# Computing the gate and up products of 15 feed-forward column blocks with the weights stationary and the tokens moving

## The chip, the cores and the metric

The kernel runs on one core of a Trainium2 chip. The metric is the device time of one execution in microseconds, the median over several runs. The trace is that of one profiled execution of the same program.

## The reference

One decoder layer on 256 tokens of width 2048, in float32: a SwiGLU feed-forward (FFN1), a token-mixing sub-layer, a second SwiGLU feed-forward (FFN2) and a last RMS norm. What the change touches is the first half of both feed-forwards, whose hidden width is 5632:

```python
def swiglu(h, w_gu, w_down):                       # h: 256 x 2048
    gate, up = jnp.split(h @ w_gu, 2, axis=-1)     # w_gu: 2048 x 11264
    return (jax.nn.silu(gate) * up) @ w_down       # w_down: 5632 x 2048
```

`x = x + 0.5 * mod * swiglu(h, ...)` is done twice, with h = modulate(rms_norm(x)). The scales and shifts of the modulation are products of one vector with a matrix of 2048 x 18432 (the conditioning), whose rows the kernel streams in beside the other work.

## The kernel before

**A product.** Every float32 operand of a large product is split in two fp32r parts, hi and lo, and a product is the sum of three: hi·hi, lo·hi, hi·lo. The activations h lie transposed in SBUF, contraction on the partitions, as `held.hi` and `held.lo` (two tiles, class `Held`, line 341), each 16 contraction steps k of 128 rows by 256 tokens. The weights come in column blocks of 512 (`CH`): `load` (line 309) brings four contraction steps, 1 MB, by one DMA on SP's queue into one of four `raw` buffers; `split` (line 330) makes of half of that (two k, 128 x 1024) `wh` by a cast on ScalarE (line 334) and `wl` by a subtraction on VectorE (line 335), into three rotating buffers each. `products` (line 319) then issues for each k and each half t of the tokens three matmuls:

```python
nc.tensor.matmul(ps, ah[:, j, ts], wh[:, j, :], start=first, stop=False)   # line 326
nc.tensor.matmul(ps, al[:, j, ts], wh[:, j, :], start=False, stop=False)   # line 327
nc.tensor.matmul(ps, ah[:, j, ts], wl[:, j, :], start=False, stop=last)    # line 328
```

The first operand, 128 x 128 of the activations, is stationary; the second, 512 columns of weights, moves. `gemm` (line 383) does so for one column block: 16 k x 2 token halves x 3 = 96 matmuls of 512 columns, into two PSUM banks (`acc_bank`, four of them), tokens on the partitions.

**The feed-forward's first half.** `ffn_up` (line 545) runs over the 11 blocks `ci` of 512 hidden columns. For each it computes the gate product, then the up product, then calls `swiglu_up` (line 525), which for each token half applies Silu to the gate's bank (ScalarE, line 537), multiplies with the up bank (VectorE, line 538) and calls `transpose_to` (line 412): four TensorE transposes of 128 x 128 (line 416) into a bank of another pool (`bank`, two of them) and a copy (line 417) into the tile that the down product reads, where the hidden columns lie on the partitions. So a block has 192 matmuls of 512 columns and eight transposes.

In FFN1 the blocks 0 to 5 go another way (`visit`, line 772: all column blocks grow together while the conditioning arrives), and `ffn_up` does the blocks 6 to 10. In FFN2 the gate product of block 0 (`head`) has been computed within the sub-layer before, and `ffn_up` does the rest of block 0 and the blocks 1 to 10.

**What sets the order.** SP's DMA queue follows the program's order. The order on TensorE, VectorE and ScalarE in these stretches is made by the framework's scheduler, which lets ready work overtake within the dependencies. Every half of a weight block calls `tick`, which now and then issues conditioning passes (line 203, VectorE) and loads of conditioning rows on SP's queue; at the end of an output of the conditioning, `gate_out` (line 266) takes a `bank`, a transpose and a ScalarE multiply. Of the remaining PSUM, two banks (`side_bank`) are used by the token mixing and the square sums, and by nothing in these blocks.

Of the kernel before, what the change touches and what calls it, by code (L numbers as in the profile page):

```python
# [9 lines left out]
F32 = mybir.dt.float32  # L10
F32R = mybir.dt.float32r
AF = mybir.ActivationFunctionType
# [4 lines left out]
P = 128  # L17
S = 256
D = 2048
DFF = 5632  # L20
NT = S // P
KD = D // P
KF = DFF // P
CH = 512
KB = 4
# [51 lines left out]
def layer_kernel(  # L77
# [22 lines left out]
    nc = tc.nc  # L100
    ctx.enter_context(tc.manual_schedule(engines={mybir.EngineType.SP}))
    b_ada = b_ada[0]
    one = ctx.enter_context(tc.tile_pool(name="one", bufs=1))
    raws = ctx.enter_context(tc.tile_pool(name="raws", bufs=RAWS))
    wsp = ctx.enter_context(tc.tile_pool(name="wsp", bufs=3))
# [10 lines left out]
    def nm(s):  # L116
        uid[0] += 1
        return f"{s}_{uid[0]}"

    def acc_bank():  # L120
        return psa.tile([P, CH], F32, tag="acc", name=nm("pa"))

    def bank():
        return psm.tile([P, CH], F32, tag="ps", name=nm("ps"))

    def side_bank():
        return psd.tile([P, CH], F32, tag="pd", name=nm("pd"))

    def t512():
        return tmp.tile([P, CH], F32, tag="t512", name=nm("t"))  # L130
# [4 lines left out]
    def slot():  # L135
        return slots.tile([P, KD * S], F32, tag="slot", name=nm("slot"))
# [154 lines left out]
    def tick():  # L291
        pace["due"] += pace["rate"]
        while pace["due"] >= 1.0:
            pace["due"] -= 1.0
            next(pace["steps"], None)
# [3 lines left out]
    def step():  # L299

        while side:
            try:
                next(side[0])
                break
            except StopIteration:
                side.pop(0)


    def load(w, kb, c0):
        raw = raws.tile([P, KB, CH], F32, tag="raw", name=nm("raw"))  # L310
        nc.sync.dma_start(
            raw,
            w[kb * KB * P : (kb + 1) * KB * P, c0 : c0 + CH].rearrange(
                "(k p) n -> p k n", p=P
            ),
        )
        return raw
# [12 lines left out]
    def split(pool, tag, src, n, hi_engine="act"):  # L330
        k = src.shape[1]
        hi = pool.tile([P, 2, n], F32R, tag=tag + "h", name=nm(tag + "h"))[:, :k, :]
        lo = pool.tile([P, 2, n], F32R, tag=tag + "l", name=nm(tag + "l"))[:, :k, :]
        nc.scalar.copy(hi, src)  # L334
        nc.vector.tensor_sub(lo, src, hi.bitcast(F32))  # L335
        return hi, lo
# [4 lines left out]
    class Held:  # L341


        def __init__(self):
            self.hi = one.tile([P, KD, S], F32R, tag="hh", name=nm("hh"))
            self.lo = one.tile([P, KD, S], F32R, tag="hl", name=nm("hl"))

        def pair(self, k2):
            return self.hi[:, 2 * k2 : 2 * k2 + 2, :], self.lo[:, 2 * k2 : 2 * k2 + 2, :]
# [20 lines left out]
    def gemm_part(act, w, col0s, banks, kb, KT):  # L370

        pairs = [act.pair(kb * 2 + h) for h in range(2)]
        for i, c0 in enumerate(col0s):
            raw = load(w, kb, c0)
            for h in range(2):
                wh, wl = split(wsp, "w", raw[:, 2 * h : 2 * h + 2, :], CH)
                ah, al = pairs[h]
                products(
                    banks[i], ah, al, wh, wl, kb + h == 0, kb * KB + 2 * h + 2 == KT
                )  # L380
                tick()

    def gemm(act, w, col0s, KT=KD):
        banks = [[acc_bank() for _ in range(NT)] for _ in col0s]
        for kb in range(KT // KB):
            gemm_part(act, w, col0s, banks, kb, KT)
            step()
        return banks
# [23 lines left out]
    def transpose_to(dest, src_of, n, ps=None):  # L412

        ps = ps or bank()
        for j in range(n):
            nc.tensor.transpose(ps[:, j * P : (j + 1) * P], src_of(j), ident)  # L416
        nc.any.tensor_copy(dest, ps[:, : n * P])  # L417
# [107 lines left out]
    def swiglu_up(banks_g, banks_u, tiles, ci, parts=None):  # L525

        k0 = ci * KB
        dest = tiles[k0 // KD].rearrange("p (k s) -> p k s", s=S)
        kk = k0 % KD
        for t in range(NT):  # L530
            s = t512()
            g, u = banks_g[t], banks_u[t]
            if parts is not None:
                nc.vector.tensor_add(s, g, parts[0][t])
                nc.vector.tensor_add(parts[1][t], u, parts[1][t])
                g, u = s, parts[1][t]
            nc.scalar.activation(s, g, AF.Silu)
            nc.vector.tensor_mul(s, s, u)
            transpose_to(
                dest[:, kk : kk + KB, t * P : (t + 1) * P],  # L540
                lambda j: s[:, j * P : (j + 1) * P],
                KB,
            )

    def ffn_up(held, w, tiles, first, bg=None):
        for ci in range(first, DFF // CH):
            bg = bg or gemm(held, w, [ci * CH])[0]
            bu = gemm(held, w, [DFF + ci * CH])[0]
            swiglu_up(bg, bu, tiles, ci)
            bg = None  # L550

    ORDERED = {mybir.EngineType.PE, mybir.EngineType.DVE, mybir.EngineType.Activation}

# [141 lines left out]
    held = Held()  # L695
    part = [slot() for _ in range(3)]
    tiles = [slot(), part[0]]
# [62 lines left out]
    banks, moved = {}, set()  # L760
# [60 lines left out]
    place = two_rows()  # L821
    set_pace([(2, None, 0.5), (4, 1, None), (3, None, None)], 154, place, AQ)
    ffn_up(held, gu, tiles, EARLY)
    gate_load(gate, 2)
    wi = w_in[0]
# [144 lines left out]
    for ci in range(4):  # L970
        b = in_chunk(O_SQ + ci * CH)
        for t in range(NT):
            u = t512()
# [10 lines left out]
    for a, off in ((0, O_RQ), (1, O_RK)):  # L984
        for ci in range(2):
            b = in_chunk(off + ci * CH)
            for t in range(NT):
                u = t512()
# [91 lines left out]
    for ci in range(4):  # L1080
        b = in_chunk(O_RG + ci * CH)
        for t in range(NT):
            u = t512()
# [12 lines left out]
    for p in range(2):  # L1096
        sg = first if p == 0 else gates(p)
        c0s = [(2 * p + i) * CH for i in range(2)]
        for g, a, w in ((1, a_swa, w_swa_branch), (0, a_ret, w_ret_branch)):
            banks = gemm(a, w[0], c0s)  # L1100
# [3 lines left out]
        for i in range(2):  # L1104
            for t in range(NT):
                m = sg[:, 0, i, t, :]
                nc.vector.tensor_add(m, m, sg[:, 1, i, t, :])
                k0 = (2 * p + i) * KB
# [12 lines left out]
    tiles = [slot() for _ in range(3)]  # L1121
    set_pace([(8, None, 0.5)], 160, raw_row, 2)
    ffn_up(held, w_ffn2_gu[0], tiles, 0, head)
    gf = one.tile([P, KD * S], F32, tag="hh", name="gf")[:, :D]
    nc.gpsimd.dma_start(gf, norm_final[None, :].broadcast_to([P, D]))
    gate_load(gate, 8)

# [80 lines left out]
```

## Time and profile before

| | us |
|---|---|
| three runs | 2444.01 to 2446.54, median 2445.94 |
| the profiled execution's own time | 2445.11 |
| its span, first to last instruction | 2443.3 |
| TensorE busy | 2398.8 (98%) |
| weight loads busy | 1957.2 (80%) |
| VectorE busy | 1699.8 (70%) |
| ScalarE busy | 1189.8 (49%) |

Times in the profile are microseconds from the first instruction of the span, durations in ns where marked. PE is TensorE's matmuls, PEld its loads of the stationary operand, DVE VectorE, ACT ScalarE, POOL GpSimd. "L335" is line 335 of the kernel. A matmul's recorded duration contains the way through the array, so consecutive ones overlap: the rate is read from the distance of their starts. PEclk is the granted share of TensorE's full clock of 2.4 GHz.

### The profile page before, as it was taken

What the parts mean: (1) busy time and instruction counts of PE and PEld (TensorE: products, weight loads), DVE (VectorE), ACT (ScalarE), POOL (GpSimd) and SP (SyncE); (2) the same over time, 40 slices, a digit from 0 to 9 for tenths busy, and PEclk for the clock granted to TensorE, in tenths of its full rate; (3) what the DMA queues carried; (4) which work ended last, traced back from release to release, by engine and by line L of the source; (5) the groups of instructions that cost most, each with busy time, mean ns of one, the idle gap of its engine ahead of it and who ended that gap; (6) DMA issues with size and microseconds to landing.
All of it is one profiled execution on the core that took longest, in us unless ns stands there. A gap on an engine that the chain in (4) does not pass through costs nothing. (4 is left out here: it accounts for less than half of the span.)

```text
span 2443.3 us, 29136 instructions
## 1 busy us (share of the span) xinstructions
PE 2398.8 (98%) x10910; PEld 1957.2 (80%) x10910; DVE 1699.8 (70%) x2733; ACT 1189.8 (49%) x1614; POOL 5.7 (0%) x14
## 2 busy tenths in 40 slices
PE   7999999999999999999999999999999999999998
PEld 4778888888787777788888888887888888888886
DVE  6898877778877677886666776767655555545656
ACT  6544544444445455554544444456544444444544
POOL 0000000000000000000000000000000000000000
PEclk9999999999999999999999999999999999999999
DMA  9987688888875766666677777755666676665563
GB/s 354 338 333 273 227 310 299 333 304 299 308 264 186 243 210 219 207 217 214 239 262 252 253 254 266 266 189 172 229 227 222 224 244 220 226 225 192 186 200 121
DMA packets 244080, 599.08 MB, mean 245 GB/s; under 512 B 9633, under 2 KB 10017, under 8 KB 225121
## 3 DMA queue, kind: packets, MB, share of 16 engines
q1 hardware_dynamic: 242434, 590.56, 69.0%
q0 software_dynamic: 928, 5.61, 0.6%
q8 instruction: 85, 1.39, 0.2%
q10 hardware_dynamic: 576, 1.05, 0.1%
q14 instruction: 57, 0.47, 0.1%
HBM read 595.06 MB, written 2.12 MB: 244 GB/s over the span
## 5 line engine op out<-in xcount | busy, mean ns | idle before, releaser
L335 DVE TENSOR_TENSOR wl<-raw,wh 128x1024 fp32r<-128x1024 f32 (+1 forms) x828 | 995.7, 1207 | 592.5 <-ACT wh L334 589.5
L334 ACT CAST wh<-raw 128x1024 fp32r<-128x1024 f32 (+1 forms) x828 | 861.2, 1041 | 1031.1 <-PE pa L327 1012.1
L326 PE MATMUL pa<-wh,hh 128*128 128x512 f32 x2224 | 870.0, 392 | 3.4 <-ACT wh L334 2.9
L327 PE MATMUL pa<-wh,hl 128*128 128x512 f32 x2224 | 869.9, 391 | 2.2 <-DVE hl L476 1.8
L328 PE MATMUL pa<-wl,hh 128*128 128x512 f32 x2224 | 803.2, 393 | 4.1 <-DVE wl L335 3.9
L326 PEld LDWEIGHTS pa<-wh,hh 128*128 128x128 f32 x2224 | 417.7, 188 | 93.3 <-ACT wh L334 4.2
L328 PEld LDWEIGHTS pa<-wl,hh 128*128 128x128 f32 x2224 | 415.3, 188 | 95.5 <-DVE wl L335 10.2
L327 PEld LDWEIGHTS pa<-wh,hl 128*128 128x128 f32 x2224 | 418.0, 188 | 89.7 <-DVE hl L476 2.4
L327 PE MATMUL pa<-wh,a 128*128 128x512 f32 x992 | 383.8, 389 | 0.0
L328 PE MATMUL pa<-wl,a 128*128 128x512 f32 x992 | 367.6, 390 | 1.2 <-DVE wl L335 1.1
L326 PE MATMUL pa<-wh,a 128*128 128x512 f32 x992 | 367.2, 390 | 0.4 <-DVE t L519 0.4
L328 PEld LDWEIGHTS pa<-wl,a 128*128 128x128 f32 x992 | 185.7, 188 | 42.3 <-DVE wl L335 4.5
L326 PEld LDWEIGHTS pa<-wh,a 128*128 128x128 f32 x992 | 186.0, 188 | 40.6 <-DVE t L519 1.1
L327 PEld LDWEIGHTS pa<-wh,a 128*128 128x128 f32 x992 | 186.3, 188 | 38.5
L203 DVE CUSTOM_DVE_ANT_0 slot<-slot,cact 128x512 f32<-128x512 f32 (+1 forms) x252 | 192.8, 814 | 31.6 <-DMA slot<-in_w_ada_dram 31.3
L203 DVE CUSTOM_DVE_ANT_0 raw<-raw,cact 128x512 f32<-128x512 f32 (+1 forms) x260 | 167.0, 696 | 38.4 <-DMA raw<-in_w_ada_dram 27.8
L367 DVE TENSOR_TENSOR a<-slot,a 128x512 fp32r<-128x512 f32 x124 | 84.8, 685 | 12.9 <-ACT a L366 12.9
L366 ACT CAST a<-slot 128x512 fp32r<-128x512 f32 x124 | 76.4, 618 | 14.8 <-PE pa L328 14.7
L417 ACT COPY slot<-ps 128x512 f32<-128x512 f32 x80 | 44.7, 586 | 38.5 <-PE ps L416 38.1
L203 DVE DVE_READ_ACCUMULATOR2_ANT sums<- 128x1 f32 x512 | 42.2, 82 | 0.0
L416 PEld LDWEIGHTS ps<-small_c,t 128*128 128x128 f32 x288 | 34.4, 140 | 7.4 <-ACT slot L955 0.7
L416 PE MATMUL ps<-small_c,t 128*128 128x128 f32 x288 | 40.1, 273 | 0.0
(161 smaller groups left out, 965.7 us busy)
## 6 DMA issues: line engine op xcount, KB each, us to landing
raw<-in_w_ffn_gu_dram SPq DMA_DIRECT2D x152, 1024.0 KB, 5.2
raw<-in_w_in_dram SPq DMA_DIRECT2D x104, 1024.0 KB, 5.2
raw<-in_w_ffn_down_dram SPq DMA_DIRECT2D x88, 1024.0 KB, 5.2
slot<-in_w_ada_dram SPq DMA_DIRECT2D x76, 1024.0 KB, 7.6
raw<-in_w_ada_dram SPq DMA_DIRECT2D x64, 1024.0 KB, 4.9
raw<-in_w_ffn_gu_dram SPq DMA_DIRECT2D x24, 768.0 KB, 6.8
raw<-in_w_swa_branch_dram SPq DMA_DIRECT2D x16, 1024.0 KB, 5.3
raw<-in_w_ret_branch_dram SPq DMA_DIRECT2D x16, 1024.0 KB, 5.3
```

Of the source, the lines that this page charges most:

```text
L203: nc.vector.tensor_tensor_reduce(out=w[:, at], in0=w[:, at], in1=cact[:, at], scale=1.0, scalar=0.0, op0=ALU.mult, op1=ALU.add, accum_out= ...
L326: nc.tensor.matmul(ps, ah[:, j, ts], wh[:, j, :], start=first, stop=False)
L327: nc.tensor.matmul(ps, al[:, j, ts], wh[:, j, :], start=False, stop=False)
L328: nc.tensor.matmul(ps, ah[:, j, ts], wl[:, j, :], start=False, stop=last)
L334: nc.scalar.copy(hi, src)
L335: nc.vector.tensor_sub(lo, src, hi.bitcast(F32))
L366: nc.scalar.copy(hi, v)
L367: nc.vector.tensor_sub(lo, v, hi.bitcast(F32))
L416: nc.tensor.transpose(ps[:, j * P : (j + 1) * P], src_of(j), ident)
L417: nc.any.tensor_copy(dest, ps[:, : n * P])
```

## The change

`Held` becomes one tile, `both`, with hi and lo side by side, so that for a given k the 256 tokens of hi and the 256 of lo can move as one operand of 512 columns. A new function `gemm_turned` computes a column block transposed: for each k and each of the four groups `o` of 128 weight columns, the group of `wh` is stationary and hi and lo move together (512 columns, one bank); then the same group of `wl` is stationary and hi moves (256 columns, added to the bank's first half). Loads, splits and ticks keep their places. Hidden columns then lie on the partitions, as the down product wants them, and the transposes fall away. The two halves of each bank are added on the way out: a ScalarE copy of the second half, a VectorE addition of the first, and then Silu (gate) or the product with the gate (up), each on 128 x 256. The gate uses the four `acc` banks, the up product two `bank`s and two `side_bank`s. The 15 blocks are 6 to 10 of FFN1 and 1 to 10 of FFN2; block 0 of FFN2 stays as it was, since its gate arrives from elsewhere.

```diff
--- before.py
+++ after.py
@@ -342,8 +342,8 @@
 
 
         def __init__(self):
-            self.hi = one.tile([P, KD, S], F32R, tag="hh", name=nm("hh"))
-            self.lo = one.tile([P, KD, S], F32R, tag="hl", name=nm("hl"))
+            self.both = one.tile([P, 2, KD, S], F32R, tag="hh", name=nm("hh"))
+            self.hi, self.lo = self.both[:, 0], self.both[:, 1]
 
         def pair(self, k2):
             return self.hi[:, 2 * k2 : 2 * k2 + 2, :], self.lo[:, 2 * k2 : 2 * k2 + 2, :]
@@ -542,12 +542,65 @@
                 KB,
             )
 
+    def gemm_turned(held, w, c0, banks):
+
+
+        for kb in range(KD // KB):
+            raw = load(w, kb, c0)
+            for half in range(2):
+                wh, wl = split(wsp, "w", raw[:, 2 * half : 2 * half + 2, :], CH)
+                for j in range(2):
+                    k = kb * KB + 2 * half + j
+                    for o, ps in enumerate(banks):
+                        os = slice(o * P, (o + 1) * P)
+
+                        def high(stop):
+                            nc.tensor.matmul(
+                                ps.rearrange("p (i s) -> p i s", i=2),
+                                wh[:, j, os],
+                                held.both[:, :, k, :],
+                                start=k == 0,
+                                stop=stop,
+                            )
+
+                        def low():
+                            nc.tensor.matmul(
+                                ps[:, :S], wl[:, j, os], held.hi[:, k, :], start=False, stop=False
+                            )
+
+                        if k < KD - 1:
+                            high(False)
+                            low()
+                        else:
+                            low()
+                            high(True)
+                tick()
+            step()
+
     def ffn_up(held, w, tiles, first, bg=None):
         for ci in range(first, DFF // CH):
-            bg = bg or gemm(held, w, [ci * CH])[0]
-            bu = gemm(held, w, [DFF + ci * CH])[0]
-            swiglu_up(bg, bu, tiles, ci)
-            bg = None
+            if bg is not None:
+                bu = gemm(held, w, [DFF + ci * CH])[0]
+                swiglu_up(bg, bu, tiles, ci)
+                bg = None
+                continue
+            bg4 = [acc_bank() for _ in range(KB)]
+            gemm_turned(held, w, ci * CH, bg4)
+            gates = [t512() for _ in range(2)]
+            gates = [gates[o // 2][:, (o % 2) * S : (o % 2 + 1) * S] for o in range(KB)]
+            for ps, s in zip(bg4, gates):
+                nc.scalar.copy(s, ps[:, S:])
+                nc.vector.tensor_add(s, s, ps[:, :S])
+                nc.scalar.activation(s, s, AF.Silu)
+            bu4 = [bank(), bank(), side_bank(), side_bank()]
+            gemm_turned(held, w, DFF + ci * CH, bu4)
+            k0 = ci * KB
+            dest = tiles[k0 // KD].rearrange("p (k s) -> p k s", s=S)
+            for o, (ps, s) in enumerate(zip(bu4, gates)):
+                u = dest[:, k0 % KD + o, :]
+                nc.scalar.copy(u, ps[:, S:])
+                nc.vector.tensor_add(u, u, ps[:, :S])
+                nc.vector.tensor_mul(u, u, s)
 
     ORDERED = {mybir.EngineType.PE, mybir.EngineType.DVE, mybir.EngineType.Activation}
 
@@ -1121,7 +1174,7 @@
     tiles = [slot() for _ in range(3)]
     set_pace([(8, None, 0.5)], 160, raw_row, 2)
     ffn_up(held, w_ffn2_gu[0], tiles, 0, head)
-    gf = one.tile([P, KD * S], F32, tag="hh", name="gf")[:, :D]
+    gf = one.tile([P, 2, KD * S], F32, tag="hh", name="gf")[:, 0, :D]
     nc.gpsimd.dma_start(gf, norm_final[None, :].broadcast_to([P, D]))
     gate_load(gate, 8)
 
```

## Rows read from the trace of the kernel before

**Rows 1.** Page, parts 1 and 2: busy time, 40 slices, granted clock

```profile
span 2443.3 us, 29136 instructions
...
PE 2398.8 (98%) x10910; PEld 1957.2 (80%) x10910; DVE 1699.8 (70%) x2733; ACT 1189.8 (49%) x1614; POOL 5.7 (0%) x14
...
PEclk9999999999999999999999999999999999999999
```

**Rows 2.** Changed stretches, FFN1, FFN2: us; PE, PEld, DVE, ACT, POOL busy; PEclk; DMA share; GB/s

```profile
308.90:530.80 221.90, 221.82 (x999) 183.65 (x998) 162.85 (x291) 94.58 (x101) 1.07 (x2) 1.00 0.84 310
1746.20:2190.50 444.30, 444.30 (x2002) 368.60 (x2001) 243.57 (x296) 190.65 (x203) 1.06 (x2) 1.00 0.66 225
```

**Rows 3.** Waits within 1725 to 2215 us, then within 310 to 560 us

```profile
ACT wh L334 <- PE pa L327: 249.6, 156, 2.1
DVE wl L335 <- ACT wh L334: 218.5, 159, 2.4
...
PEld pa L328 <- DVE wl L335: 0.5, 1, 0.5
```

**Rows 4.** Timeline, PE, 1787.6 to 1797 us: start, duration, instruction

```profile
1787.62 0.39 PE L326 MATMUL pa<-wh,hh 128*128 128x512 f32 x1
...
1795.32 0.40 PE L327 MATMUL pa<-wh,hl 128*128 128x512 f32 x1
1795.55 1.04 PE L416 MATMUL ps<-small_c,t 128*128 128x128 f32 x8
1796.35 0.48 PE L328 MATMUL pa<-wl,hh 128*128 128x512 f32 x1
1796.67 0.39 PE L326 MATMUL pa<-wh,hh 128*128 128x512 f32 x1
```

**Rows 5.** Timeline, ACT: the first Silu of blocks 7, 8 (FFN1), 6, 7 (FFN2)

```profile
375.01 0.60 ACT L537 ACTIVATE t<-pa 128x512 f32<-128x512 f32 x1 [1.21 <-PE pa L328]
...
419.45 0.60 ACT L537 ACTIVATE t<-pa 128x512 f32<-128x512 f32 x1 [1.21 <-PE pa L328]
...
1990.91 0.60 ACT L537 ACTIVATE t<-pa 128x512 f32<-128x512 f32 x1 [1.21 <-PE pa L328]
...
2035.33 0.60 ACT L537 ACTIVATE t<-pa 128x512 f32<-128x512 f32 x1 [1.21 <-PE pa L328]
```

**Rows 6.** Timeline, weight loads, the same place as rows 4

```profile
1796.32 0.19 PEld L328 LDWEIGHTS pa<-wl,hh 128*128 128x128 f32 x1
1796.43 0.19 PEld L326 LDWEIGHTS pa<-wh,hh 128*128 128x128 f32 x1
1796.67 0.19 PEld L327 LDWEIGHTS pa<-wh,hl 128*128 128x128 f32 x1
```

**Rows 7.** Timeline, PE, 1117.7 to 1119.5 us: float32 matmuls of 256 columns

```profile
1117.69 0.59 PE L1032 MATMUL pd<-slot,t 128*128 128x256 f32 x2
1118.12 0.59 PE L1033 MATMUL pd<-slot,t 128*128 128x256 f32 x2
```

**Rows 8.** By line: operations of swiglu_up (512 columns), then of 256 columns

```profile
L537 ACT ACTIVATE t<-pa x32: 597/598/600, 330.6 to 2170.2; 128x512 f32<-128x512 f32 x32
L417 ACT COPY slot<-ps x80: 563/587/597, 258.5 to 2196.7; 128x512 f32<-128x512 f32 x80
L538 DVE TENSOR_TENSOR t<-t,pa x32: 676/686/689, 354.8 to 2191.2; 128x512 f32<-128x512 f32 x32
...
L955 ACT COPY slot<-ps x16: 350/373/375, 888.4 to 1108.9; 128x256 f32<-128x256 f32 x16
L1040 ACT ACTIVATE t<-pd x16: 377/382/387, 1110.4 to 1188.7; 128x256 f32<-128x256 f32 x16
L476 DVE TENSOR_TENSOR hl<-t,hh x16: 411/420/426, 26.0 to 240.6; 128x256 fp32r<-128x256 f32 x16
```

**Rows 9.** Timeline, DVE, where the changed blocks begin in FFN1 and FFN2

```profile
309.06 1.28 DVE L535 TENSOR_TENSOR slot<-pa,slot 128x512 f32<-128x512 f32 x2
...
1746.11 1.37 DVE L538 TENSOR_TENSOR t<-t,pa 128x512 f32<-128x512 f32 x2
```

## The prediction

> **What bounds the kernel now.** I read the page first. TensorE is busy for 98% of the span and its clock is granted in full in all slices, the 2.4 GHz level [rows 1]. Busy time of pipelined matmuls overlaps, though, so that share alone proves nothing; what proves it is the distance of starts in the stretch that changes. In a piece without transposes, from 1787.62 to 1795.32 us, lie 34 matmul distances [rows 4]: 7.70 / 34 = 0.2265 us, to within the rounding of the rows. A block has 192 such matmuls and eight transposes. Those stand between two products of 512 columns at 1795.32 and 1796.67 [rows 4]; between the two lie one more product and the transposes, so they cost 1.35 - 2 x 0.2265 = 0.897 us. The product right behind them shows a start that is too early and a duration that is too long (1796.35 and 0.48), so it isn't used. 192 x 0.2265 + 0.90 = 44.38 us; the distance of the first Silu in neighbouring blocks is 44.44 us in FFN1 and 44.42 us in FFN2 [rows 5]. The other way round, (44.42 - 0.90) / 192 = 0.2267 us, which I use below. Nothing is left over: in these blocks the time is the rate of TensorE, and no wait ends last.
>
> The other engines have room. In the changed stretches, 666.2 us together, VectorE is busy for 73% in FFN1 and 55% in FFN2, ScalarE for 43% in both [rows 2]. ScalarE's casts wait for TensorE to free a buffer, VectorE's subtractions wait for the casts, and in FFN1 the weight loads waited for `wl` just once, 0.5 us [rows 3].
>
> **The change, part by part.**
>
> *Transposes.* 15 blocks lose eight transposes each: 15 x 0.897 = 13.5 us off the path.
>
> *The products.* The columns that move are as many as before: 64 x (512 + 256) = 49152 for a product against 96 x 512 = 49152. But there are 128 matmuls for 96, half of them 256 columns wide, each with a stationary operand of its own. So the path takes 128 matmuls of 0.2267 us and 128 of p for a block, and all hangs on p. At half of 0.2267 it is 0.1133 and the products cost what they did. There are 128 x 15 = 1920 narrow matmuls, so each ns on p is 1.92 us.
>
> No row shows an fp32r matmul of 256 columns. The neighbours: plain float32 matmuls of 256 columns follow each other after (1118.12 - 1117.69) / 2 = 0.215 us [rows 7]. That is 256 columns at half the rate of 2.4 GHz, 0.2133, and some 2 ns, so a fixed cost of a matmul with its weights can be as low as 2 ns. An fp32r matmul of 512 columns takes 0.2267 against 512 / 2.4 = 213.3 ns, 13.3 ns more, and the trace doesn't say if that is by matmul or by column. If by column, p is 0.1133; if by matmul, 106.7 + 13.3 = 0.120. The load of the next weights must fit beside a narrow matmul as well. Recorded it takes 0.19 us, which would make p at least that: 1920 x 0.077 = 147 us slower. The row excludes it: behind the transposes, two loads of fp32r weights start 0.11 us apart, at 1796.32 and 1796.43, though each is recorded with 0.19 [rows 6]. So the load is worth 0.11, with a few ns of hand-over. I take p = 0.115, just above both the pro-rata value and the load: 1920 x 0.0017 = 3.2 us. The ends kept for the range are 0.110 (-6.4 us) and 0.129 (below, +30 us).
>
> The Trainium skill ("TensorE: Matmul & The Clock Gate", section "LDWEIGHTS (loading the stationary operand)") puts a load at its number of columns over 1.2 GHz, 107 ns for 128. The 0.11 us between the loads agrees. By that figure alone the load would bind nowhere, p would be 0.1133, and the sum would be 3.2 us lower.
>
> *On the way out of PSUM.* A block loses two Silus (0.60), two copies (0.59) and two multiplications (0.69) of 512 columns, and gets, with 256 columns, eight copies and four Silus on ScalarE and eight additions and four multiplications on VectorE [rows 8]. ScalarE: 8 x 0.37 + 4 x 0.38 - 2.37 = +2.1 us; VectorE: 12 x 0.42 - 1.37 = +3.7 us. Over 44 us, VectorE goes to about 82% in FFN1 and 64% in FFN2. None of it is on the path: gate and up use eight banks by turns, so a bank has a whole product, some 22 us, to be emptied before it is written again, and the last up product is followed by a down product that starts with other tiles and the gate's banks. What hides it is the lead of the splits; if that goes, the price is a late `wl`, below. I put it at nothing.
>
> *Banks at the seams.* The first gate product of each stretch wants four `acc` banks at once, where two sufficed. Two of them are still being read: in FFN1 by the additions of line 535 (309.06 us, two, 1.28 us), in FFN2 by the multiplications of line 538 (1746.11 us, two, 1.37 us) [rows 9]. TensorE has the other two groups to go on with for 2 x (0.227 + 0.115) = 0.7 us, or twice that if the second k is drawn ahead. And the transpose of `gate_out`, which falls at the end of the last gate product of FFN2 (64 passes over 160 halves), now shares its pool with the up banks. Three places of 0 to 1.4 us: I take 1.5 us in all.
>
> *Nothing* for: the loads (same DMAs, order and ticks on SP's queue; POOL's load of the final gain waits for the same last product as before); hi and lo in one tile (written before these blocks begin).
>
> Sum: -13.5 + 3.2 + 1.5 = -8.8 us. The profiled execution took 2445.11 us, 0.83 below the median of the runs; 2445.11 - 8.8 + 0.83 = 2437.1, rounded to **2437 us**. A difference of 0.2%, 4.9 us, is about what a measurement of this kernel can tell from none.
>
> **The rivals.**
>
> *The excess is by matmul.* Then p = 0.120: 1920 x 6.7 ns = 12.8 us, and -13.5 + 12.8 + 1.5 = +0.8, 2447 us: the added instructions eat what the transposes give. For it: each matmul has its own load, and the load starts within 0.01 us of the matmul before it, so something at each matmul is plausible. Against: plain float32, with a load for each matmul too, shows 2 ns [rows 7]. Chance 0.30. The Trainium skill (the same page, "Back-to-back issue gap") has a fixed cost by matmul, 2.5 ns, over N / 2.4. By its form the rival holds; its figure disagrees with the 13.3 ns here, and by the figure p would be 0.109, under the load's 0.11.
>
> *The load binds, and slower than read (the slower side).* The 0.11 was seen when no fp32r operand was moving at full rate. If the two hinder each other, and the load is slowed by what the wide matmul loses, p = 0.1155 + 0.0133 = 0.129: 1920 x 0.0157 = 30.1 us, -13.5 + 30.1 + 1.5 = +18, 2464 us. It decides from p = 0.1195 on, where the sum is nothing, and is plainly slower above 0.122. For it: the narrow matmul leaves the load no slack. Against: in the transposes, a load and 128 moving columns go side by side in 0.897 / 8 = 0.11 us [rows 4]. Chance 0.15.
>
> *Emptying delays the weights in FFN1.* With VectorE at 82% and up to 3.4 us of its work coming due at the end of an up product, one subtraction (1.2 us) late for each of the ten products of FFN1 is 12 us: -8.8 + 12 = +3, 2449 us. Against: three buffers, and waits of casts for TensorE in nearly every half [rows 3]. Chance 0.05.
>
> *The narrow product isn't cheaper.* If it takes 0.227 whatever its width, 1920 x 0.1133 = 218 us slower, 2652 us. Against: the transposes, 128 columns, at 0.11 us each [rows 4] and plain float32 at 0.215 for 256 [rows 7]. Chance 0.02.
>
> **How the numbers follow.** The forecast has 0.48, and all its spread of p (0.110 to 0.117) is faster by over 4.9 us or near it. The rivals at 2447 and 2449 lie within 0.2%: 0.30 + 0.05 = 0.35. Slower: 0.15 + 0.02 = 0.17. The range goes from 2431 (p near 0.112 and no seams) to 2456 (p = 0.125, part of the slower rival) and leaves out under 0.2. The likeliest case's own range is 2431 to 2442.
>
> **What would show it.** In the changed kernel: distance of starts of a wide and a narrow matmul together 0.342 us (0.347 if by matmul, 0.356 if the load binds); blocks 43.8 us apart, 44.4 or 45.4 in the rivals; no line 416 in these blocks; casts still waiting for TensorE; gaps before the first matmuls of block 6 in FFN1 and block 1 in FFN2 of at most 1.4 us. I am wrong if the pair takes over 0.347 us, or if loads wait for `wl`.

## The result, and the profile after

The changed kernel takes 2452.17 us (median of 10 runs, 2449.84 to 2453.8) against 2446.61 us for the kernel before (10 runs): a ratio of 1.0023, 95% interval 1.0013 to 1.0033. It is slower by 5.6 us; the forecast was 2437 us, faster by 0.4%. The profiled execution took 2453.6 us, 1.4 above its median, and that of before 2445.11 us, 1.5 below the median of those ten runs, so the two traces differ by more (8.5 us of span) than the medians.

The page of the changed kernel, parts 1 and 2, answers to [rows 1]:

```profile
span 2451.8 us, 31098 instructions
...
PE 2406.2 (98%) x11750; PEld 1992.7 (81%) x11750; DVE 1740.4 (71%) x2883; ACT 1215.8 (50%) x1734; POOL 5.7 (0%) x14
...
PEclk9999999999999999999999999999999999999999
```

The clock is as before. There are 840 more matmuls: 15 x 64 added, 15 x 8 transposes removed. The changed stretches, FFN1 and then FFN2, with the columns of [rows 2]:

```profile
308.10:534.70 226.60, 225.72 (x1292) 196.54 (x1291) 175.25 (x337) 104.59 (x142) 1.07 (x2) 1.00 0.83 307
1750.10:2200.30 450.20, 450.20 (x2572) 392.37 (x2571) 269.70 (x392) 208.94 (x284) 1.06 (x2) 1.00 0.66 222
```

They have grown from 221.9 and 444.3 us, and TensorE is still busy in all of them; VectorE stands at 77% and 60%, ScalarE at 46%. The timeline of ScalarE gives the blocks, as in [rows 5]: the first Silu of block 1 and that of block 10 in FFN2, nine blocks apart (the scheduler moves single Silus by up to 2 us, so neighbours won't do here):

```profile
1773.97 0.42 ACT L594 ACTIVATE t<-t 128x256 f32<-128x256 f32 x1
...
2178.17 0.42 ACT L594 ACTIVATE t<-t 128x256 f32<-128x256 f32 x1
```

404.20 / 9 = 44.91 us a block. Before the change it was 44.42 from one block to the next, and 44.44 over nine blocks of FFN2, among which one small transpose of `gate_out` falls; 43.8 was forecast. The timeline of PE says where it lies. Line 558 is the wide matmul, 567 the narrow one; the columns are those of [rows 4]:

```profile
1805.86 0.40 PE L558 MATMUL pa<-hh,wh 128*128 128x512 f32 x1
1806.09 0.28 PE L567 MATMUL pa<-hh,wl 128*128 128x256 f32 x1
1806.21 0.40 PE L558 MATMUL pa<-hh,wh 128*128 128x512 f32 x1
1806.44 0.28 PE L567 MATMUL pa<-hh,wl 128*128 128x256 f32 x1
...
1808.68 0.40 PE L558 MATMUL pa<-hh,wh 128*128 128x512 f32 x1
```

Eight pairs from 1805.86 to 1808.68 us: 0.3525 us a pair. From the first to the last of the 2560 matmuls of the FFN2 stretch it is 0.3507 (449.79 us, less 0.87 for the eight transposes of block 0 that fall among them, over 1280). The columns alone, at the rate of before, make 0.2267 + 0.1133 = 0.3400. By their starts, the narrow matmul goes on for 0.117 us and the wide one for 0.234. The forecast had 0.342, and a pair over 0.347 was its sign of being wrong.

One more thing lies on the path: in FFN1 a narrow matmul once waited for its weights.

```profile
409.18 0.74 PE L567 MATMUL pa<-hh,wl 128*128 128x256 f32 x4 [0.88 <-DVE wl L335]
```

The distance of starts there is 1.28 us in place of 0.23, so 1.0 us is lost. The cast that this `wl` needs had ended at 405.52 us; VectorE had the emptying of PSUM to do until 405.46 and then four conditioning passes (line 203) until 407.90, before it began the subtraction. At the seams nothing waits. The terms as the trace has them: pairs 1920 x 0.0107 = +20.5 (the loss of a pair as FFN2 shows it), transposes -13.5 (the run without them, below), the late weights +1.0, together +8.0 of the 8.5 us between the two spans.

### The profile page after: what moved, and what is told of

It reads as the page before. It is cut to its first block, busy times and chain, and to the rows that moved or that the text cites. A ratio compares the mean times of both kernels' runs of the same rounds, so it can differ in the third digit from the quotient of the medians.

```text
span 2451.8 us, 31098 instructions
## 1 busy us (share of the span) xinstructions
PE 2406.2 (98%) x11750; PEld 1992.7 (81%) x11750; DVE 1740.4 (71%) x2883; ACT 1215.8 (50%) x1734; POOL 5.7 (0%) x14
## 5 line engine op out<-in xcount | busy, mean ns | idle before, releaser
L326 PE MATMUL pa<-wh,hh 128*128 128x512 f32 x1264 | 496.5, 395 | 3.4 <-ACT wh L334 2.8
L327 PE MATMUL pa<-wh,hh 128*128 128x512 f32 x1264 | 496.3, 393 | 2.3 <-DVE hh L476 1.9
L328 PE MATMUL pa<-wl,hh 128*128 128x512 f32 x1264 | 463.4, 394 | 4.0 <-DVE wl L335 3.9
L558 PE MATMUL pa<-hh,wh 128*128 128x512 f32 x960 | 324.5, 396 | 0.0
L326 PEld LDWEIGHTS pa<-wh,hh 128*128 128x128 f32 x1264 | 237.6, 188 | 56.0 <-ACT wh L334 4.1
L328 PEld LDWEIGHTS pa<-wl,hh 128*128 128x128 f32 x1264 | 235.6, 188 | 58.1 <-DVE wl L335 9.7
L327 PEld LDWEIGHTS pa<-wh,hh 128*128 128x128 f32 x1264 | 237.9, 188 | 52.6 <-DVE hh L476 2.5
L567 PE MATMUL pa<-hh,wl 128*128 128x256 f32 x960 | 244.0, 281 | 0.9 <-DVE wl L335 0.9
L558 PEld LDWEIGHTS pa<-hh,wh 128*128 128x128 f32 x960 | 176.5, 188 | 37.0
L567 PEld LDWEIGHTS pa<-hh,wl 128*128 128x128 f32 x960 | 174.9, 189 | 7.4 <-DVE wl L335 1.3
L558 PE MATMUL pd<-hh,wh 128*128 128x512 f32 x480 | 174.4, 395 | 0.0
L558 PE MATMUL ps<-hh,wh 128*128 128x512 f32 x480 | 173.2, 396 | 0.0
```

The lines of the kernel that those rows point to most:

```text
L558: nc.tensor.matmul(ps.rearrange("p (i s) -> p i s", i=2), wh[:, j, os], held.both[:, :, k, :], start=k == 0, stop=stop,)
L567: nc.tensor.matmul(ps[:, :S], wl[:, j, os], held.hi[:, k, :], start=False, stop=False)
```

## The experiments

Three theories stood against each other for what a pair loses: the extra time of an fp32r matmul over its columns is spent by matmul, whatever its load; the load of the next stationary operand binds beside a narrow matmul; the two runs of the wide matmul's moving operand cost. The pair times below are taken over the same 1280 pairs of FFN2 in each kernel, from the first start to the last, as above; the granted clock was 0.998 to 0.999 of full in all of these traces. The times of x1, x4, x5, x8, y1 and y3 are those of a single execution, so these kernels are read by their pairs. The edits are shown abridged, against the changed kernel; that of the transposes is against the kernel before.

| kernel | wide, narrow columns; columns of a load | order | pair, us | columns alone | kernel, us |
|---|---|---|---|---|---|
| changed | 512, 256; 128 | by turns | 0.3507 | 0.3400 | 2452.17 |
| x1_low_128 | 512, 128; 128 | by turns | 0.3409 | 0.2833 | 2434.30 |
| x4_cols_64 | 512, 256; 64 | by turns | 0.3414 | 0.3400 | 2438.32 |
| x2_grouped | 512, 256; 128 | 8 and 8 | 0.3489 | 0.3400 | 2447.74 |
| x3_one_run | 512, 256; 128 | by turns | 0.3507 | 0.3400 | 2452.17 |
| x5_low_384 | 512, 384; 128 | by turns | 0.4123 | 0.3967 | 2569.11 |
| y1_low_384_cols_64 | 512, 384; 64 | by turns | 0.4038 | 0.3967 | 2554.98 |
| y3_low_512 | 512, 512; 128 | by turns | 0.4533 | 0.4533 | 2648.81 |
| x8_grouped_192 | 512, 192; 128 | 8 and 8 | 0.3398 | 0.3117 | 2431.54 |

**A narrower narrow matmul.**

```diff
-  ps[:, :S], wl[:, j, os], held.hi[:, k, :],
+  ps[:, :P], wl[:, j, os], held.hi[:, k, :P],
```

> The narrow matmul moves only the tokens 0 to 127 (128 columns); the hi x lo-weight term of the other tokens is left out. In the changed kernel a wide matmul goes on for 0.234 us and a narrow one for 0.117. Theory 'by matmul' (each fp32r matmul costs 13.3 ns over its columns, whatever its load): the narrow one falls to 53.3 + 13.3 = 0.067, the pair to about 0.30, a block from 44.9 to about 38.5 us. Theory 'the load binds' (while a narrow matmul runs, the next stationary operand needs 0.11 to 0.12 us to load): the narrow one stays at 0.11 to 0.12 and the block at 44 to 45 us.

The timeline of PE in this kernel:

```profile
1900.32 0.45 PE L558 MATMUL pd<-hh,wh 128*128 128x512 f32 x1
1900.60 0.22 PE L567 MATMUL pd<-hh,wl 128*128 128x128 f32 x1
1900.66 0.45 PE L558 MATMUL pd<-hh,wh 128*128 128x512 f32 x1
...
1902.36 0.67 PE L558 MATMUL ps<-hh,wh 128*128 128x512 f32 x2
```

Six pairs in 2.04 us, 0.340 each. The narrow matmul's start comes late and the wide one's early (0.45 us recorded for it), so only the pair counts: 0.3409 - 0.2267 = 0.114 us for 128 columns, whose stream takes half of that. "By matmul" wanted a pair of about 0.30 and falls. Half the columns gave back only 0.010 of 0.124 us: below that there is a floor that doesn't go by the moving columns, and of the three theories only the load's has one. In runs of narrow matmuls in this trace, the starts are 0.111 apart.

**A shorter load.** The stationary operand has 64 columns; the rows left out are set to zero (GpSimd), and the way out of PSUM handles 64 partitions.

```diff
-  os = slice(o * P, (o + 1) * P)
+  os = slice(o * P, o * P + 64)
-  ps.rearrange("p (i s) -> p i s", i=2), wh[:, j, os],
+  ps[:64].rearrange("p (i s) -> p i s", i=2), wh[:, j, os],
```

> The stationary operand has 64 columns in place of 128, so half of each group's hidden columns are left out (their rows in the tile that the down product reads are set to zero by GpSimd). The moving columns stay: 512 and 256. Theory 'by matmul': nothing changes but the loss at the change of widths, narrow 0.117 to 0.120, wide 0.227 to 0.234. Theory 'the load binds': the load takes half, the narrow one falls to 0.107 to 0.113 and the wide one, no longer delayed, to 0.227; pair 0.340, block 43.5 us. Third theory, 'the load takes time from the moving columns, by its own columns': the 13.3 ns fall to half, wide 0.220, narrow 0.113, pair 0.333, block 42.6 us.

```profile
1902.09 0.39 PE L558 MATMUL ps<-hh,wh 128*64 128x512 f32 x1
1902.32 0.28 PE L567 MATMUL ps<-hh,wl 128*64 128x256 f32 x1
...
1903.12 0.39 PE L558 MATMUL pd<-hh,wh 128*64 128x512 f32 x1
```

Three pairs in 1.03 us; over the stretch 0.3414 a pair, the wide matmul at 0.228 and the narrow at 0.1135. With half the load nearly the whole loss is gone, though the moving columns are the same. Half the load also means half the rows written to PSUM, which this run can't tell from the load. With bfloat16 operands (below), narrow matmuls that write all 128 rows run at 0.1133 too, so the rows alone don't cost the time; but there the type changes as well. And 0.1135 is 256/512 of 0.2267, to 0.2 ns: the 13.3 ns that an fp32r matmul of 512 columns takes over 512 / 2.4 go by moving column, neither by matmul nor by the load's columns, which would have made the wide one 0.220. The Trainium skill ("TensorE: Matmul & The Clock Gate", section "Step-by-step: what each phase is for") says that loading the next weights takes no read bandwidth from the running matmul. Whether it is read bandwidth that load and stream share, no run here shows; in time the two are not independent for fp32r operands, since at 256 moving columns a load of 128 columns costs 0.3507 us a pair and one of 64 costs 0.3414.

**Order.** Eight wide matmuls, then eight narrow ones.

```diff
+  final = kb == KD // KB - 1 and half == 1
+  for part in (low, high) if final else (high, low):
+      for j, o in [(j, o) for j in range(2) for o in range(KB)]:
+          part(j, o)
```

> Order alone: of each half of a weight block the eight wide matmuls go first, then the eight narrow ones (the last half the other way round); the same matmuls. If the change of widths costs (as the trace of the changed kernel has it: 0.234 for a wide one behind a narrow one, 0.228 to 0.230 behind a wide one; 0.1194 for a narrow one among narrow ones), a pair falls from 0.351 to about 0.348, a block to 44.5 us, the kernel by 15 x 0.4 = 6 us to about 2446 us, level with the kernel before. If order is nothing, 2452 us.

```profile
1900.71 2.08 PE L566 MATMUL pa<-hh,wl 128*128 128x256 f32 x16
1902.62 2.00 PE L556 MATMUL pa<-hh,wh 128*128 128x512 f32 x8
1904.46 0.62 PE L556 MATMUL ps<-hh,wh 128*128 128x512 f32 x2
```

Sixteen narrow ones in 1.91 us, 0.1194 each; eight wide ones behind them in 1.84, 0.230 each. The pair falls to 0.3489, and the kernel to 2447.74 us, 4.4 below the changed one and level with the kernel before (1.0008, 0.9999 to 1.0017). In a run of narrow matmuls alone, each takes 0.1194 to 0.120 where its columns need 0.1133: that part of the loss belongs to the narrow matmul beside a full load, the rest to the change of widths.

**One run of moving columns.** hi and lo of a k side by side.

```diff
-  self.both = one.tile([P, 2, KD, S], F32R, tag="hh", name=nm("hh"))
+  self.both = one.tile([P, KD, 2, S], F32R, tag="hh", name=nm("hh"))
```

> hi and lo of one k lie next to each other in SBUF, so that the wide matmul's 512 moving columns are one run and not two of 256. If the two runs make the wide one slower (0.234 against 0.227 in the kernel before), it falls to 0.227, the pair to 0.344, the kernel by 1920 x 7 ns = 13 us to about 2439 us. If the excess comes from widths or loads, nothing changes: 2452 us.

2452.17 us (1.0027, 1.0017 to 1.0037), the pair unchanged at 0.3507. That the wide operand moves as two runs of 256 columns costs nothing.

**Wider, and equal.** The narrow matmul with 384 columns, with full and with half loads (hi and lo lie in one run there, as above), and with 512. These kernels add terms that neither kernel has, so their times say nothing of the change; their pairs do.

```diff
-  ps[:, :S], wl[:, j, os], held.hi[:, k, :],
+  ps[:, : S + P], wl[:, j, os], held.both[:, k].rearrange("p i s -> p (i s)")[:, : S + P],
```

> The narrow matmul moves 384 columns (hi, and 128 tokens of lo, which adds a small term that neither kernel has). hi and lo lie in one run. Theory now: the fp32r stream takes 13.3 ns per 512 columns by column, and a 128-column load beside it needs about 0.120 us, so it is late only behind a matmul shorter than that. Then the 384-column matmul takes 384 x 0.4427 = 0.170 us, the wide one 0.2267, no loss: pair 0.397. Rival: alternating widths costs by itself; then the wide one stays at 0.234 and the pair is 0.404 or more.

> The 384-column kernel (wide 512, narrow 384, by turns, 0.413 us a pair where the columns alone give 0.397) with stationary operands of 64 columns (half of each group's hidden columns left out, zeros in their place). If what a pair loses comes of a 128-column load and the stream hindering each other, it goes, as it did at 512 and 256: wide 0.227, narrow 0.170, pair 0.397. If the change of widths costs by itself, the pair stays at 0.413.

> Both matmuls move 512 columns (hi and lo with either weight part; the lo x lo term is added that neither kernel has). Everything else as in the changed kernel: weights stationary, four banks by turns, 128 loads a product. If the turned form costs nothing by itself and only unequal widths do, every matmul takes 0.2267 as in the kernel before and a block 256 x 0.2267 = 58.0 us. If stationary weights or the turn of banks cost, more: 0.230 or above, 59 us.

The PE timeline with 384 columns and full loads:

```profile
1901.06 0.39 PE L558 MATMUL pa<-hh,wh 128*128 128x512 f32 x1
1901.29 0.34 PE L567 MATMUL pa<-hh,wl 128*128 128x384 f32 x1
...
1903.12 0.40 PE L558 MATMUL pa<-hh,wh 128*128 128x512 f32 x1
```

and with 512 columns in both:

```profile
1900.45 0.39 PE L558 MATMUL pa<-hh,wh 128*128 128x512 f32 x1
1900.68 0.39 PE L567 MATMUL pa<-hh,wl 128*128 128x512 f32 x1
...
1902.95 0.39 PE L558 MATMUL pd<-hh,wh 128*128 128x512 f32 x1
```

The first was a miss for the theory that a load is only late behind a matmul shorter than itself: five pairs in 2.06 us, 0.412, though 0.170 us of columns would cover a load of 0.11 to 0.12. The pair loses 0.0156. With loads of 64 columns 0.0071 of that is left, so over half of it hangs on the load here too. What the rest hangs on isn't shown: unequal widths alone don't explain it, for at 512 and 256 the half loads left only 0.0014. With equal widths of 512 nothing is lost: eleven matmuls in 2.50 us, 0.2267 over the stretch, as before the change. So stationary weights, the turn of four banks and 128 loads a product cost nothing by themselves.

**The load's own time.** The grouped order with 192 of the 256 tokens in the narrow matmul.

```diff
-  banks[o][:, :S], wl[:, j, o * P : (o + 1) * P], held.hi[:, k, :],
+  banks[o][:, :192], wl[:, j, o * P : (o + 1) * P], held.hi[:, k, :192],
```

> Grouped order, and the narrow matmuls move 192 of 256 tokens (the hi x lo-weight term of the other 64 is left out). Runs of narrow matmuls took 0.112 us each at 128 columns and 0.1199 at 256. If the load is slowed by the time that columns stream beside it, 192 columns give about 0.116; if it is 0.112 until the stream itself fills that time, 0.112. With the stream as the bound it would be 192 x 0.4427 = 0.085, which is excluded if the load binds.

```profile
1900.00 0.39 PE L566 MATMUL pd<-hh,wl 128*128 128x192 f32 x2
...
1900.45 0.38 PE L566 MATMUL pd<-hh,wl 128*128 128x192 f32 x2
```

Four in 0.45 us; over the stretch they take 0.112 us each in runs, where 192 columns alone would take 0.085 and where 128 columns took 0.111. So 0.112 is a floor that up to 192 moving columns don't change, and it is read here as the load with its hand-over (no run has a shorter load and fewer columns at once, so a floor of another kind is not excluded); at 256, where the columns want 0.1133, it becomes 0.120. The Trainium skill ("TensorE: Matmul & The Clock Gate", section "LDWEIGHTS (loading the stationary operand)") puts a load at its number of columns over 1.2, which by the page's figure is an estimate of 107 ns for 128 columns. The 0.112 here is within 5 ns of that.

**The transposes.** The kernel before, without them and their copies in the 15 blocks; the product goes untransposed to the down product's tile.

```diff
+  if flat:
+      s4, u4 = (v.rearrange("p (k s) -> p k s", s=P) for v in (s, u))
+      nc.vector.tensor_mul(to, s4, u4)
+      continue
```

> The kernel before, with the transposes of the 15 blocks left out (the product of gate and up is written to the down product's tile untransposed, and the copies go too). This measures the first term of the sum alone: 15 x 0.897 = 13.5 us, to about 2432 us. If transposes hide in gaps of TensorE, less.

```profile
1983.27 0.60 ACT L537 ACTIVATE t<-pa 128x512 f32<-128x512 f32 x1 [1.22 <-PE pa L328]
...
2026.79 0.60 ACT L537 ACTIVATE t<-pa 128x512 f32<-128x512 f32 x1 [1.22 <-PE pa L328]
```

2431.45 us (0.9937, 0.9922 to 0.9952): 14.3 us below the kernel before, measured beside it. The distance of the first Silu in neighbouring blocks of FFN2 goes down to 43.52 us from the 44.42 of [rows 5], so 15 x 0.90 = 13.5 us by the trace. They hid nowhere.

**Longer groups.** Sixteen and sixteen.

```diff
+  for part in (low, high) if final else (high, low):
+      for k in range(kb * KB, (kb + 1) * KB):
+          for o in range(KB):
+              part(k, o)
```

> The changed kernel with groups of 16 wide matmuls, then 16 narrow ones (a whole block of four k). In the grouped order with eight, a group loses about 18 ns more than its matmuls in long runs (0.2267 and 0.1199) would; with half as many changes, a pair falls from 0.348 to about 0.347 us, the kernel by about 2 us to 2445 or 2446 us, level with the kernel before. The floor of this way is 128 x (0.2267 + 0.1199) = 44.37 us a block against 44.42 before, so no order of it wins. If the weight buffers (three) don't feed groups of this length, gaps appear and it is slower.

2449.45 us (1.0014, 1.0005 to 1.0023), no better than groups of eight. The pair came down by about what was expected: over the stretch it is 0.3486, but that counts 0.93 us of down-product matmuls that the scheduler put among the last narrow ones, and without them it is 0.348 against 0.3489. The 2 us that this should give did not come out in the kernel's time. In the two traces the difference lies where neither kernel was changed: between the last matmul of the changed FFN1 blocks and the first of FFN2's pass 1216.1 us here and 1213.7 with groups of eight. Why, and whether the 1.7 us between the medians come from there, is not settled.

**Narrow matmuls in bfloat16.** Both operands of the narrow matmuls are read as bfloat16, the upper halves of the same words; the term hi x lo-weights is coarser for it.

```diff
+  def upper(v):
+      return v.bitcast(BF16)[:, 1::2]
-  wl[:, j, o * P : (o + 1) * P], held.hi[:, k, :],
+  upper(wl[:, j, o * P : (o + 1) * P]), upper(held.hi[:, k, :]),
```

> The grouped order, and both operands of the narrow matmuls are read as bfloat16: the upper 16 bits of the same fp32r values in place (step of two elements), so nothing is added. That coarsens only the term hi x lo-weights. If the runs of narrow matmuls (0.1199 us each) are held up by the loads of fp32r weights, a load of half the bytes frees them: 0.1133 or less, pair about 0.341, block 43.7 us, kernel 2436 to 2440 us, faster than both. If the load's time goes by columns whatever their bytes, or the step of two costs as much as it saves, they stay at 0.120 and the kernel at 2447 to 2448 us.

> The same reading of the narrow matmuls' operands, in the changed kernel's order (wide and narrow by turns). Here the load beside a narrow matmul is that of the next wide one, which is fp32r as before. If that load binds, the pair stays near 0.351 and the kernel at 2450 to 2452 us, though its own load is cheaper. If what counts is the narrow matmul's own operands, the pair falls to about 0.342 and the kernel to about 2437 us.

In the grouped order:

```profile
1903.19 0.40 PE L571 MATMUL ps<-hh,wl 128*128 128x256 bf16 x2
1903.43 0.39 PE L571 MATMUL pd<-hh,wl 128*128 128x256 bf16 x2
1903.66 0.39 PE L571 MATMUL ps<-hh,wl 128*128 128x256 bf16 x2
1903.88 0.39 PE L571 MATMUL pd<-hh,wl 128*128 128x256 bf16 x2
1904.02 0.72 PE L561 MATMUL ps<-hh,wh 128*128 128x512 f32 x2
...
1905.97 0.40 PE L571 MATMUL ps<-hh,wl 128*128 128x256 bf16 x2
```

The narrow matmuls follow each other after 0.1133 us over the stretch (here four in 0.45, from 1903.43 to 1903.88), no longer 0.120. Since both operands changed, the run doesn't tell if the lighter load or the other stream brought that. The change of type costs more than that of widths, so the pair is 0.3456 over the stretch (the eight pairs from 1903.19 to 1905.97 take 2.78 us, 0.3475 each) and not 0.341. The kernel takes 2442.45 us (0.9982, 0.9973 to 0.9991): 3.6 us below the kernel before and 9.7 below the changed one, faster than both, if less than expected. By turns the change of type is paid in every pair: 0.358, 2467.35 us (1.0087, 1.0073 to 1.0101), slower than either theory had it.

## Why the prediction was wrong

*What bounds the kernel* was right: TensorE's rate before and after, with the other engines aside.

*The transposes* were right: -13.5 us forecast, -13.5 by the blocks and -14.3 by the kernel's time in the run without them.

*The products: the step that failed.* "I take p = 0.115, just above both the pro-rata value and the load." Over the old wide matmul, the pair took 0.124. The reading by column was right (0.1135 with half loads), and so was the load alone (0.112, as it is read above); wrong was to take little more than the larger of the two, as if load and stream ran side by side without a price. A load of 128 fp32r columns beside 256 fp32r columns gives 0.120, and with widths by turns another 4 ns a pair, most of it seen in the wide matmul, which the prediction took to cost what it did. 1920 x (0.1240 - 0.1150) = 17 us, against a forecast gain of 8.8. The measured 2452 us lies within the stated range only at its slow end, which had been kept open for a part of the slower rival; the forecast direction was wrong.

One reading behind that step was loose. The two lines of [rows 7] are not four float32 matmuls: line 1032 issues eight matmuls in all, one for each head, and the trace has 16 of them with 16 loads. So each is recorded as two passes, and the 0.215 us belong to a pass of 256 columns, while a whole float32 matmul takes 0.43. That a load beside such a pass can cost as little as 2 ns stands, but the pass leaves 0.215 us for the load, where the fp32r matmul leaves 0.1133, and so the row said little about the narrow matmul.

*The rivals.* The second one, that the load binds and is slower beside a full-rate stream, comes nearest to what happened: it put p at 0.129, called the kernel plainly slower above 0.122, and gave 2464 us at a chance of 0.15. It sized the hindrance with the 13.3 ns of the wide matmul, which turned out to belong to the moving columns; measured, it is 8 ns over the load's 0.112 and 4 for the turns. "By matmul" would have given 0.120 for the narrow one too, and runs of narrow matmuls show just that, but the half loads exclude it. That a narrow product isn't cheaper is excluded by the pairs.

*Seams*: 1.5 us forecast, nothing measured; the wider gaps near both seams are the transposes of the block before. *Emptying*: put at nothing, and true but for one late `wl` in FFN1, 1.0 us. VectorE grew by 2.5 to 2.6 us a block where 3.7 was worked out from single durations.

How load and stream hinder each other, and why a pair of 512 and 384 columns loses 0.0156 us though the load has time there, the runs don't show; that stays open.

## What to carry to other kernels

Where a rewrite keeps the moving columns and cuts them into unequal matmuls, count with a price for each pair: 0.0107 us at 512 and 256 here, and 0.0156 at 512 and 384, where the load had time to spare. Ask first if the next stationary operand can be loaded beside the narrow ones, and don't take "just fits" for "free". Equal widths of 512 columns ran at the old rate with the operands' parts exchanged. If narrow ones can't be avoided, group them, and see whether their operands may be of a narrower type; in groups, for by turns the narrower type took 2467 us against 2442.

## What was not expected of the hardware

An fp32r matmul's time over its columns at 2.4 GHz goes by moving column (0.2267 us for 512, 0.1135 for 256 with a load of 64). Reading two operands as bfloat16 in place, with a step of two elements, brought 256 columns in a run from 0.120 to 0.1133 us, no further, though a column at 2.4 GHz would need 0.107. Fp32r and bfloat16 matmuls by turns took 0.358 us a pair against 0.346 in groups of eight.
